# A hybrid decoder layer on one core: output projection at 512 columns, spread table building, gate weights through shared buffers, softmax division on ScalarE

## The chip, the cores and the metric

The kernel runs on one core of one Trainium2 chip. The metric is the device time in microseconds (us) of one execution, all loads and stores included. TensorE is the matmul engine, VectorE, ScalarE and GpSimd are the three elementwise engines, and SyncE (SP) issues the DMAs. The profile calls them PE (and PEld for its weight loads), DVE, ACT, POOL and SP.

## What is computed

The input x has 2048 positions of 1024 channels. It is normalised, projected to 2816 columns, worked on in three head groups, projected back with `w_out`, added to x and normalised again. Cut to what matters:

```python
hn = rmsnorm(x, norm_g)
a_in, a_gate, c_in, c_b, c_c, c_gate, q, q_gate = split(hn @ w_in)   # 384 x6, 256 x2
# A: 24 groups of a diagonal complex state-space model with 64 states, then GELU and a gated unit
s = associative_scan(lam_bar, b_bar @ a_in)
g = gelu(Re(C s) + d * a_in)
y_ssm = g * sigmoid(g @ w_glu + b_glu) * silu(a_gate)
# B: short causal convolution of width 3
y_conv = c_b * conv3(c_c * c_in) * silu(c_gate)
# M: attention of 4 heads of 64 into 256 memory rows
k, v = split(rmsnorm(mem, mem_norm_g) @ w_mem_kv)
y_mem = softmax(q k^T / 8) v * silu(q_gate)
h = x + concat(y_ssm, y_conv, y_mem) @ w_out                          # 1024 x 1024
out = rmsnorm(h, final_norm_g)
```

All data is float32. Matrix products are made from two-part operands: each operand is split into a rounded part (`hi`) and the rest (`lo`), and `mm3` (line 79) issues three matmuls: hi*hi, hi*lo and lo*hi.

## The kernel before, in words

**Quarters and stages.** The 2048 positions are cut into four quarters of 512. For each quarter `prep` (line 582) normalises x in four row blocks of 128 and transposes them into `hn`, channels on partitions. `proj` (line 606) makes one block of 128 output columns of the input projection: it loads a 1024 x 128 weight tile, splits it, and issues 8 x 3 matmuls with 512 columns (positions) into one PSUM tile. `ain`, `agate`, `qproj` and `conv` are loops over such blocks with their elementwise work. `attention(q, j)` (line 760) does two heads: scores into PSUM, row maximum on VectorE (line 778), exponential with a row sum on ScalarE (line 780), a reciprocal (line 782) and the division of the four 128 x 256 blocks by the row sum on VectorE (line 785), then transposes (line 795), the split into two parts, and the product with v (line 799). `ssm(hf)` (line 480) runs the state-space model over half the positions, eight steps of three groups each; its scan is a chain on VectorE that ends in `sC`, which TensorE reads at line 548. `glu(q)` (line 813) reads the result of `ssm` back from DRAM, splits it into `y_ssm`, and multiplies by `w_glu` in three column blocks of 128 (line 830). `outproj` and `outproj_last` (lines 893, 921) are the output projection.

**Output projection.** The weights of a matmul (stationary operand) are 128 positions of an output slice Y, its moving operand is a piece of `w_out`. `wout` (line 889) loads 512 rows x 256 columns of it and splits it. `outproj` loops over four column blocks, two halves of the rows, and four row blocks of positions; `omm` (line 866) then issues 4 k x 3 matmuls of 256 columns. Two PSUM tiles hold two row blocks each and are added to the reloaded x by VectorE (line 905). Quarters are finished in the order 1, 0, 3, 2. Quarter 2 comes last, in `outproj_last`, which loads all eight weight tiles ahead into buffers that have come free: three of the projections' buffers, the rest of `hn`'s, v's (`wvd`), a table's (`wtb`), and the conv and memory outputs' (`wyc`, `wym`). It does row blocks 0 and 1 together, then 2, then 3. Its conv and memory outputs have been reloaded from DRAM into `hn`'s buffer (`hy`, in `fetch_y`, line 848), as were those of quarter 0 into buffers of their own.

**Buffers.** `wtile` (line 127) loads a weight tile into a staging tile, rounds it on ScalarE (`split`, line 86) and makes the rest on GpSimd or VectorE (line 77). Staging `w` has two buffers, `wl`, the split weights, three. The tiles of `w_glu` are staged in the pair of buffers `ain`, which `glu` also uses for its input `gr`, and split into a buffer `wg` of its own, one deep. `xst` (tag `x`) holds two row blocks of x, and also the sets of turns below. PSUM has three tiles `mm`, two `tr`, one `po` (attention's product with v) and two `ss`, one bank each.

**Tables.** In the first quarter the kernel also builds the tables of the state-space model: four tables (`gen_table`, line 392, five steps each, six large VectorE operations) and eight sets of turns (`gen_turns`, line 442, one step each, six products and two sums on VectorE, then a store to `t_dram`). They follow `mem_rows` (four steps), which normalises the memory rows. Ahead of them `ssm_prologue` derives their parameters in many small operations.

**What sets the order.** The generators yield after each step, and `interleave(main, side, rate, start)` (line 676) advances `side` by `rate` steps for each step of `main`; `merge` does the same within one stream. This order gives each instruction its rank. A planner in the compiler then lays out each engine's instructions by rank and by its own estimate of when their inputs and buffers are ready. On the chip each engine and SP's queue run in that fixed order. Lines 1002 to 1026 write the stages out. The first quarter's: `agate(0)`, `qproj(0)`, `conv(0, 0)`, `conv(0, 1)` (15 steps) with `mem_rows` and all tables (32 steps) at a rate of 2.2, then `conv(0, 2)` and `memory_kv` with `prep(1)`.

Of the kernel before, what the change touches and what calls it, by code (L numbers as in the profile page):

```python
# [9 lines left out]
F32 = mybir.dt.float32  # L10
F32R = mybir.dt.float32r
# [34 lines left out]
def hymba_layer_kernel(  # L46
# [29 lines left out]
    def tt(o, a, b, op, e=V):  # L76
        e.tensor_tensor(o, a, b, op)  # L77
# [598 lines left out]
    def interleave(main, side, rate, start=0):  # L676
# [8 lines left out]
        for _ in side:  # L685
            pass

    def merge(a, b, rate):

        acc = 0.0  # L690
        for _ in a:
            yield
            acc += rate
            while acc >= 1.0:
                acc -= 1.0
                if next(b, 0) is None:
                    yield
        yield from b
# [61 lines left out]
    def attention(q, j):  # L760
# [5 lines left out]
        for ip in range(2):  # L766
# [15 lines left out]
            V.reciprocal(sm, sm)  # L782
            for a in range(2):
                for h in range(2):
                    V.tensor_scalar(pe[:, a, h], pe[:, a, h], sm[:, a, h:h + 1], None, ALU.mult)
                pes.append(pe[:, a])
            yield
        um = yv["pe"][:, 0].rearrange("p (a h m) -> p a h m", a=2, h=2)[:, :, 0]
# [24 lines left out]
    def glu(q):  # L813
# [13 lines left out]
            split(y_ssm[:, 0, t], y_ssm[:, 1, t], gr)  # L827
            yield
        for m in range(3):
            w = wtile(w_glu[0, :, m * P:(m + 1) * P], WS, P, f"wg{q}{m}", V, late["wg"], "a")  # L830
            ps = ps_ss.tile([P, QL], F32, tag="ss", name=f"psg{q}{m}")
            for k in range(3):
                mm3(ps, w[:, 0, k, :], w[:, 1, k, :], y_ssm[:, 0, k, :], y_ssm[:, 1, k, :], k == 0, k == 2)
            t_, g2 = (swk.tile([P, QL], F32, tag="pg", bufs=2, name=f"gt{q}{m}{z}") for z in range(2))
            S.activation(t_, ps, AF.Tanh, bias=bg[:, m:m + 1], scale=0.25)
            tt(g2, f32(y_ssm[:, 0, m, :]), f32(y_ssm[:, 1, m, :]), ALU.add, G)
            V.scalar_tensor_tensor(g2, t_, 1.0, g2, ALU.add, ALU.mult)
            V.scalar_tensor_tensor(us[m], g2, 0.125, us[m], ALU.mult, ALU.mult)
            yield
# [2 lines left out]
        yield  # L842


    yk = [("ssm", 0), ("ssm", 1), ("ssm", 2), ("conv", 0), ("conv", 1), ("mem", 0), ("mem", 1), ("conv", 2)]
    rows = [0, 1, 2, 3, 4, 6, 7, 5]

    def fetch_y(q):

# [13 lines left out]
                t = Y[q]["conv" if z + k < 3 else "mem"][:, :, (z + k) % 3]  # L863
                split(t[:, 0], t[:, 1], st[:, k], V if k else G)

    def omm(q, ps, i, kh, w, first):

        o_ = slice(i * P, (i + 1) * P)
        for k in range(4):
            nm, kk = yk[4 * kh + k]  # L870
            kr = rows[4 * kh + k] - 4 * kh
            mm3(ps, Y[q][nm][:, 0, kk, o_], Y[q][nm][:, 1, kk, o_], w[:, 0, kr, :], w[:, 1, kr, :],
                first and k == 0, kh == 1 and k == 3, skip_group_check=True)

    def residual(q, last=False):

# [9 lines left out]
                nc.sync.dma_start(h[z][u * NCH:(u + 1) * NCH], xq[q, u][:, 2 * z:2 * z + 2])  # L886
        return h

    def wout(q, n_, kh, dst=None, st="w", e=G):
        src = w_out[0, kh * 512:(kh + 1) * 512, n_ * 256:(n_ + 1) * 256]  # L890
        return wtile(src, 512, 256, f"wo{q}{n_}{kh}", e, dst, st)

    def outproj(q):
        h = residual(q)
        for n_ in range(4):
            ns = slice(n_ * 256, (n_ + 1) * 256)
            pss = [ps_mm.tile([P, 2, 256], F32, tag="mm", name=f"po{q}{n_}{b}") for b in range(2)]
            for kh in range(2):
                w = wout(q, n_, kh)
                for i in range(4):  # L900
                    omm(q, pss[i // 2][:, i % 2, :], i, kh, w, kh == 0 and i % 2 == 0)
                    yield
            for b in range(2):
                hb = h[b][:, :, ns]
                tt(hb, pss[b], hb, ALU.add)
        jk = tmp.tile([P, QL], F32, tag="ci", name=f"junk{q}")
        ss = sml.tile([P, 2, 4], F32, tag="ssf", name=f"ssf{q}")
        for i in range(4):
# [12 lines left out]
    def outproj_last(q):  # L921
# [4 lines left out]
        hg = late["big"].tile([P, 2, DM], F32, tag="big1", name="hg")  # L926

        def wv_(t):
            return t[:, :2 * 4 * 256].rearrange("p (z k n) -> p z k n", z=2, k=4)

        dsts = [None, None, None, Y[q]["rest"].rearrange("p z a (b n) -> p z (a b) n", b=2)]
        dsts.append(wv_(kvp.tile([P, 2 * 4 * 256], F32R, tag="vd", name="wvd")))
        dsts.append(wv_(stab.tile([P, GB * TW], F32, tag="tb", name="wtb").bitcast(F32R)))
        dsts.append(wv_(late["yc"].tile([P, 2 * 3 * QL], F32R, tag="yc", name="wyc")))
        dsts.append(wv_(late["ym"].tile([P, 2 * 2 * QL], F32R, tag="ym", name="wym")))
        ws = [[wout(q, n_, kh, dsts[2 * n_ + kh], "wx"[kh], V if kh else G) for kh in range(2)] for n_ in range(4)]
        ss, jk = (sml.tile([P, 4, 4], F32, tag=t_, bufs=1, name=t_) for t_ in ("ssl", "ssk"))

        def rstd(i, nss):
# [8 lines left out]
        for n_ in range(4):  # L948
            ns = slice(n_ * 256, (n_ + 1) * 256)
            ps = ps_mm.tile([P, 2, 256], F32, tag="mm", name=f"po{q}{n_}")  # L950
            for kh in range(2):
                for i in range(2):
                    omm(q, ps[:, i, :], i, kh, ws[n_][kh], kh == 0 and i == 0)
            for i in range(2):
                tt(h[i][:, ns], ps[:, i], h[i][:, ns], ALU.add)
                sumsq(h[i][:, ns], ss[:, i, n_:n_ + 1], junk[0][:, 0:256])
        for i in range(2):
            V.scalar_tensor_tensor(h[i], h[i], rstd(i, 4), fg_b, ALU.mult, ALU.mult)
            store(i, h[i])
        for i in range(2, 4):  # L960
            parts = [(0, 1), (2, 3)] if i == 2 else [(0, 1), (2,), (3,)]
            for b, ns_ in enumerate(parts):
                ns = slice(ns_[0] * 256, ns_[-1] * 256 + 256)
                ps = ps_mm.tile([P, 2, 256], F32, tag="mm", name=f"po{q}{i}_{b}")
                for a, n_ in enumerate(ns_):
                    for kh in range(2):
                        omm(q, ps[:, a, :], i, kh, ws[n_][kh], kh == 0 and a == 0)
                pv = ps.rearrange("p a n -> p (a n)")[:, :256 * len(ns_)]
                tt(h[i][:, ns], pv, h[i][:, ns], ALU.add)
                sumsq(h[i][:, ns], ss[:, i, b:b + 1], junk[1][:, :256 * len(ns_)])  # L970
# [10 lines left out]

    def open_left():
        phs.close()
        for n_ in ("yc", "ym", "wg"):
            late[n_] = ctx.enter_context(tc.tile_pool(name=n_, bufs=1, reuse_waits="tile"))

    prologue = ssm_prologue()
# [15 lines left out]
    open_right()  # L1003
    load_small()
    gens = chain(*[z for b in range(NB) for z in (gen_table(b), gen_turns(2 * b), gen_turns(2 * b + 1))])
    kv = memory_kv()
    interleave(chain(agate(0), qproj(0), conv(0, 0), conv(0, 1)), chain(mem_rows(), gens), 2.2)
    open_left()
    interleave(merge(conv(0, 2), kv, 0.7), prep(1), 2.0, 4)
    interleave(ain(1), chain(attention(0, 0), attention(0, 1)), 2.5)  # L1010

    def main(q):
# [43 lines left out]
```

## Time and profile before

| what | us |
|---|---|
| median of 3 runs | 902.94 (900.92 to 909.04) |
| the profiled execution | 904.45 |
| its span, first to last instruction | 902.5 |
| TensorE busy in the span | 843.1 |
| VectorE busy | 613.7 |
| ScalarE busy | 367.0 |
| GpSimd busy | 301.7 |

Times in rows are microseconds from the span's start unless marked ns. `x24` after a group is its number of instructions; what follows the bar is busy time and the mean ns of one, then the engine's idle time just before them and what ended it. Matmuls overlap in their pipeline, so the duration of one is longer than the distance to the next start.

### The profile page before, as it was taken

The numbers are of one execution on the slowest core, as the hardware profiler recorded it, in microseconds if no ns is written. First come the engines' busy times: TensorE is split into PE (matmuls) and PEld (weight loads), VectorE is DVE, ScalarE is ACT, GpSimd is POOL, SyncE is SP. The second block draws the span as 40 slices with busy tenths as digits, with TensorE's granted clock in tenths as the row PEclk, the third lists the DMA queues.
The fourth block names the chain that finished last, engine by engine and source line by source line (L and its number), as shares of the span: only waits on it lengthen the run. The fifth ranks groups of instructions, "written<-read, shape, count | busy, mean of one in ns | idle before, by whom it ended". The sixth has DMA issues, their size and how long they took to land. (4 is left out here: it accounts for less than half of the span.)

```text
span 902.5 us, 13173 instructions
## 1 busy us (share of the span) xinstructions
PE 843.1 (93%) x4876; PEld 723.7 (80%) x4876; DVE 613.7 (68%) x1244; ACT 367.0 (41%) x706; POOL 301.7 (33%) x157
## 2 busy tenths in 40 slices
PE   2998999889998998999999899999999998989996
PEld 2985777778877877899888688899878876879996
DVE  6898899583998896936434664344399996865353
ACT  5343433545343434433444533335233344444511
POOL 2000001154222344444545434334443343455400
PEclk9999899999997999999999999999999999999999
DMA  9553649966464534454575632656757744493362
GB/s 205 161 150 103 189 131 269 267 187 201 125 179 130 156 93 119 108 152 141 159 239 150 160 114 84 161 165 186 214 156 207 211 128 125 117 222 112 125 177 57
DMA packets 180647, 142.97 MB, mean 158 GB/s; under 512 B 41192, under 2 KB 164584, under 8 KB 180584
## 3 DMA queue, kind: packets, MB, share of 16 engines
q1 hardware_dynamic: 180584, 142.14, 56.4%
q8 instruction: 38, 0.62, 0.3%
q14 instruction: 25, 0.20, 0.1%
HBM read 113.80 MB, written 26.74 MB: 156 GB/s over the span
## 5 line engine op out<-in xcount | busy, mean ns | idle before, releaser
L77 POOL TENSOR_TENSOR wo<-wo_st,wo 128x1024 fp32r<-128x1024 f32 x26 | 63.8, 2454 | 70.6 <-ACT wo L86 59.2
L77 DVE TENSOR_TENSOR h<-po,h 128x512 f32<-128x512 f32 (+1 forms) x37 | 22.2, 615 | 43.5 <-PE po L83 34.5
L81 PE MATMUL po<-wo,yssm 128*128 128x256 f32 x168 | 48.5, 289 | 1.8 <-ACT yssm L86 1.8
L83 PE MATMUL po<-wo,yssm 128*128 128x256 f32 x168 | 48.2, 287 | 0.0
L82 PE MATMUL po<-wo,yssm 128*128 128x256 f32 x168 | 47.8, 285 | 0.0
L780 ACT ACTIVATE pe<-sps,nm 128x256 f32<-128x256 f32 x64 | 29.5, 472 | 39.4 <-DVE nm L778 35.1
L81 PE MATMUL psai<-hn,wai 128*128 128x512 f32 (+1 forms) x120 | 42.7, 362 | 2.8 <-ACT hn L86 2.1
L82 PE MATMUL psai<-hn,wai 128*128 128x512 f32 (+1 forms) x120 | 42.5, 356 | 0.3 <-DVE hn L77 0.2
L83 PE MATMUL psai<-hn,wai 128*128 128x512 f32 (+1 forms) x120 | 42.0, 353 | 0.0
L81 PE MATMUL pscg<-hn,wcg 128*128 128x512 f32 x96 | 39.8, 415 | 2.2 <-ACT wcg L86 2.2
L86 ACT CAST wo<-wo_st 128x1024 fp32r<-128x1024 f32 x27 | 28.2, 1044 | 33.3 <-PE po L83 16.2
L81 PE MATMUL po<-wo,yconv 128*128 128x256 f32 x144 | 40.7, 283 | 0.0
L83 PE MATMUL po<-wo,yconv 128*128 128x256 f32 x144 | 40.3, 280 | 0.0
L82 PE MATMUL po<-wo,yconv 128*128 128x256 f32 x144 | 40.1, 279 | 0.0
L83 PE MATMUL pscg<-hn,wcg 128*128 128x512 f32 x96 | 39.1, 407 | 0.5 <-DVE wcg L77 0.5
L81 PE MATMUL psag<-hn,wag 128*128 128x512 f32 x96 | 39.5, 411 | 0.0
L82 PE MATMUL pscg<-hn,wcg 128*128 128x512 f32 x96 | 39.0, 407 | 0.0
L77 POOL TENSOR_TENSOR wcb<-wcb_st,wcb 128x1024 fp32r<-128x1024 f32 x9 | 22.9, 2550 | 47.9 <-ACT wcb L86 47.9
L83 PE MATMUL psag<-hn,wag 128*128 128x512 f32 x96 | 38.5, 401 | 0.0
L82 PE MATMUL psag<-hn,wag 128*128 128x512 f32 x96 | 38.4, 400 | 0.0
L81 PE MATMUL pscb<-hn,wcb 128*128 128x512 f32 x96 | 38.3, 399 | 0.0
L81 PE MATMUL psci<-hn,wci 128*128 128x512 f32 x96 | 38.3, 399 | 0.0
(710 smaller groups left out, 2903.5 us busy)
## 6 DMA issues: line engine op xcount, KB each, us to landing
wo_st<-in_w_out_dram SPq DMA_DIRECT2D x32, 512.0 KB, 3.8
tb<-t_dram SPq DMA_DIRECT2D x16, 960.0 KB, 5.5
out_dram<-h SPq DMA_DIRECT2D x32, 256.0 KB, 3.4
h<-in_x_dram SPq DMA_DIRECT2D x14, 512.0 KB, 7.4
wai_st<-in_w_in_dram SPq DMA_DIRECT2D x12, 512.0 KB, 4.3
wag_st<-in_w_in_dram SPq DMA_DIRECT2D x12, 512.0 KB, 4.3
wci_st<-in_w_in_dram SPq DMA_DIRECT2D x12, 512.0 KB, 4.2
wcc_st<-in_w_in_dram SPq DMA_DIRECT2D x12, 512.0 KB, 4.1
```

Of the source, the lines that this page charges most:

```text
L77: e.tensor_tensor(o, a, b, op)
L81: T.matmul(ps, lh, rh, start=first, stop=False, **kw)
L82: T.matmul(ps, lh, rl, start=False, stop=False, **kw)
L83: T.matmul(ps, ll, rh, start=False, stop=last, **kw)
L86: S.copy(hi, src)
L780: S.activation(pe[:, a, h], sps[h][:, a], AF.Exp, bias=nm_[:, a, h:h + 1], accum_out=sm[:, a, h:h + 1])
```

## The change

Four edits. The output projection works with 512 columns and 256 rows of `w_out` per tile, in four row pairs taken in the order 0, 1, 3, 2, with four accumulators (three `mm`, one `po`); the last quarter likewise, except that its very last column half stays in two pieces of 256. The division of the softmax is an ACTIVATE on ScalarE. `w_glu` comes in two tiles, of 256 and 128 columns, through staging `w` and buffers `wl`. The tables go alongside the first four main pieces at a rate of 1.5 instead of 2.2; the rest runs at 0.9 beside `conv(0, 2)` and `memory_kv`, where `prep(1)` runs too, and what is left of it follows `prep(1)`.

```diff
+    def weave(main, side, rate):
+        acc = 0.0
+        for _ in main:
+            acc += rate
+            while acc >= 1.0:
+                acc -= 1.0
+                next(side, None)
+            yield
...
-                    V.tensor_scalar(pe[:, a, h], pe[:, a, h], sm[:, a, h:h + 1], None, ALU.mult)
+                    S.activation(pe[:, a, h], pe[:, a, h], AF.Copy, scale=sm[:, a, h:h + 1])
...
         for m in range(3):
-            w = wtile(w_glu[0, :, m * P:(m + 1) * P], WS, P, f"wg{q}{m}", V, late["wg"], "a")
+            if m % 2 == 0:
+                c1 = min(m * P + 256, WS)
+                wg = wtile(w_glu[0, :, m * P:c1], WS, c1 - m * P, f"wg{q}{m}", V)
+            w = wg[:, :, :, m % 2 * P:m % 2 * P + P]
...
-    yk = [("ssm", 0), ("ssm", 1), ("ssm", 2), ("conv", 0), ("conv", 1), ("mem", 0), ("mem", 1), ("conv", 2)]
-    rows = [0, 1, 2, 3, 4, 6, 7, 5]
+    yk = [("ssm", 0), ("ssm", 1), ("ssm", 2), ("conv", 0), ("conv", 1), ("conv", 2), ("mem", 0), ("mem", 1)]
+    pairs = (0, 1, 3, 2)
...
-    def omm(q, ps, i, kh, w, first):
+    def omm(q, ps, i, kp, w, cs=slice(0, 512)):
         o_ = slice(i * P, (i + 1) * P)
-        for k in range(4):
-            nm, kk = yk[4 * kh + k]
-            kr = rows[4 * kh + k] - 4 * kh
-            mm3(ps, Y[q][nm][:, 0, kk, o_], Y[q][nm][:, 1, kk, o_], w[:, 0, kr, :], w[:, 1, kr, :],
-                first and k == 0, kh == 1 and k == 3, skip_group_check=True)
+        for k in range(2):
+            nm, kk = yk[2 * kp + k]
+            mm3(ps, Y[q][nm][:, 0, kk, o_], Y[q][nm][:, 1, kk, o_], w[:, 0, k, cs], w[:, 1, k, cs],
+                kp == pairs[0] and k == 0, kp == pairs[-1] and k == 1)
...
-    def wout(q, n_, kh, dst=None, st="w", e=G):
-        src = w_out[0, kh * 512:(kh + 1) * 512, n_ * 256:(n_ + 1) * 256]
-        return wtile(src, 512, 256, f"wo{q}{n_}{kh}", e, dst, st)
+    def wout(q, nh, kp, dst=None, st="w", e=G):
+        src = w_out[0, kp * 256:(kp + 1) * 256, nh * 512:(nh + 1) * 512]
+        return wtile(src, 256, 512, f"wo{q}{nh}{kp}", e, dst, st)
...
-        for n_ in range(4):
-            ns = slice(n_ * 256, (n_ + 1) * 256)
-            pss = [ps_mm.tile([P, 2, 256], F32, tag="mm", name=f"po{q}{n_}{b}") for b in range(2)]
-            for kh in range(2):
-                w = wout(q, n_, kh)
+        for nh in range(2):
+            ns = slice(nh * 512, (nh + 1) * 512)
+            pss = [ps_mm.tile([P, 512], F32, tag="mm", name=f"po{q}{nh}{b}") for b in range(3)]
+            pss.append(ps_po.tile([P, QL], F32, tag="po", name=f"po{q}{nh}3"))
+            for kp in pairs:
+                w = wout(q, nh, kp)
                 for i in range(4):
-                    omm(q, pss[i // 2][:, i % 2, :], i, kh, w, kh == 0 and i % 2 == 0)
+                    omm(q, pss[i], i, kp, w)
                     yield
-            for b in range(2):
-                hb = h[b][:, :, ns]
-                tt(hb, pss[b], hb, ALU.add)
+            for i in range(4):
+                hb = h[i // 2][:, i % 2, ns]
+                tt(hb, pss[i], hb, ALU.add)
...
-        for n_ in ("yc", "ym", "wg"):
+        for n_ in ("yc", "ym"):
...
-    kv = memory_kv()
-    interleave(chain(agate(0), qproj(0), conv(0, 0), conv(0, 1)), chain(mem_rows(), gens), 2.2)
+    side = chain(mem_rows(), gens)
+    for _ in weave(chain(agate(0), qproj(0), conv(0, 0), conv(0, 1)), side, 1.5):
+        pass
+    interleave(weave(merge(conv(0, 2), memory_kv(), 0.7), side, 0.9), prep(1), 2.0, 4)
+    for _ in side:
+        pass
     open_left()
-    interleave(merge(conv(0, 2), kv, 0.7), prep(1), 2.0, 4)
```

`outproj_last` is changed in the same way: weight tiles of 256 x 512 into the same eight buffers, two column halves for row blocks 0 and 1, and for row block 3 the pieces 0 to 512, 512 to 768 and 768 to 1024.

## Rows read from the trace of the kernel before

**Rows 1.** The page, part 1: busy us, share of the span, instructions.
```profile
PE 843.1 (93%) x4876; PEld 723.7 (80%) x4876; DVE 613.7 (68%) x1244; ACT 367.0 (41%) x706; POOL 301.7 (33%) x157
```

**Rows 2.** Who waited for whom, TensorE: total us, times, longest.
```profile
PE ps_y L548 <- DVE sC L77: 9.9, 6, 3.1
PE psg L81 <- ACT wg L86: 8.0, 4, 3.4
PE trq L144 <- DVE hn L77: 4.1, 2, 2.8
PE psqg L81 <- DVE uq L619: 4.1, 1, 4.1
PE pscg L81 <- ACT wcg L86: 2.2, 1, 2.2
...
PE po L81 <- ACT yssm L86: 1.8, 1, 1.8
```

**Rows 3.** Order of time, TensorE, 377 to 383: start, duration, line, tiles.
```profile
378.07 0.39 PE L83 MATMUL pscg<-hn,wcg 128*128 128x512 f32 x1
...
380.79 0.39 PE L83 MATMUL pscg<-hn,wcg 128*128 128x512 f32 x1
381.01 0.28 PE L81 MATMUL po<-wo,yssm 128*128 128x256 f32 x1
...
382.33 0.28 PE L83 MATMUL po<-wo,yssm 128*128 128x256 f32 x1
```

**Rows 4.** Order of time, TensorE, 842 to 850, in the last stage.
```profile
843.16 0.28 PE L83 MATMUL po<-wo,yconv 128*128 128x256 f32 x1
...
845.20 0.28 PE L83 MATMUL po<-wo,ymem 128*128 128x256 f32 x1
...
849.45 0.28 PE L81 MATMUL po<-wo,hy 128*128 128x256 f32 x1
...
849.69 0.28 PE L83 MATMUL po<-wo,hy 128*128 128x256 f32 x1
```

**Rows 5.** Stretches: length, busy PE, PEld, DVE, ACT, POOL, clock, DMA share, GB/s.
```profile
80.00:100.00 20.00, 14.66 (x79) 10.12 (x79) 14.84 (x51) 7.80 (x13) 1.10 (x2) 0.74 0.57 137
150.00:200.00 50.00, 44.85 (x253) 38.36 (x253) 37.32 (x70) 23.50 (x48) 18.79 (x10) 0.97 0.86 232
200.00:220.00 20.00, 20.00 (x100) 16.29 (x99) 5.90 (x16) 10.36 (x25) 8.04 (x4) 1.00 0.81 235
270.00:290.00 20.00, 16.88 (x76) 14.29 (x75) 17.72 (x40) 8.67 (x23) 3.76 (x2) 0.74 0.47 134
760.00:810.00 50.00, 44.08 (x239) 37.05 (x235) 32.94 (x42) 23.82 (x44) 27.31 (x15) 0.93 0.68 168
```

**Rows 6.** VectorE by line and shape: count, busy us, mean ns, idle before.
```profile
L785 DVE TENSOR_SCALAR pe<-pe,sm 128x256 f32<-128x256 f32 x64 | 29.4, 524 | 0.2
...
L77 DVE TENSOR_TENSOR ge<-t0e,t1e 128x384 f32<-128x384 f32 x16 | 9.8, 652 | 0.6 <-DMA t_dram<-ge 0.5
...
L77 DVE TENSOR_TENSOR t0e<-s_U,s_W 128x256 f32<-128x256 f32 x24 | 8.7, 415 | 0.5 <-ACT s_W L330 0.5
...
L77 DVE TENSOR_TENSOR gt<-gt 128x768 f32<-128x768 f32 x8 | 7.5, 954 | 0.0
```

**Rows 7.** Line 785: count, then minimum, median and maximum ns.
```profile
L785 DVE TENSOR_SCALAR pe<-pe,sm x64: 341/349/2544, 206.6 to 769.6; 128x256 f32<-128x256 f32 x64
```

**Rows 8.** ScalarE by line and shape, 845 to the end.
```profile
L101 ACT ACTIVATE junkci<-h 128x256 f32<-128x256 f32 x8 | 3.3, 418 | 11.9 <-DVE h L77 11.7
```

**Rows 9.** Order of time, ScalarE, 760 to 766.
```profile
763.07 0.62 ACT L86 CAST yssm<-gr 128x512 fp32r<-128x512 f32 x1 [3.08 <-DMA gr<-g_dram]
763.63 0.51 ACT L86 CAST wg<-wg_st 128x384 fp32r<-128x384 f32 x1
```

**Rows 10.** Order of time, DMA issues on SP, 795 to 806.
```profile
797.43 2.01 SPq L823 DMA_DIRECT2D us<-y_dram  x3
799.53 4.23 SPq L131 DMA_DIRECT2D wg_st<-in_w_glu_dram  x2
```

More of the change, by code (lines that the diff above doesn't have):

```diff
@@ L928, in wv_ @@
         def wv_(t):
-            return t[:, :2 * 4 * 256].rearrange("p (z k n) -> p z k n", z=2, k=4)
-        dsts = [None, None, None, Y[q]["rest"].rearrange("p z a (b n) -> p z (a b) n", b=2)]
-        dsts.append(wv_(kvp.tile([P, 2 * 4 * 256], F32R, tag="vd", name="wvd")))
+            return t[:, :2 * 2 * 512].rearrange("p (z k n) -> p z k n", z=2, k=2)
+        dsts = [None, None, None, Y[q]["rest"]]
+        dsts.append(wv_(kvp.tile([P, 2 * 2 * 512], F32R, tag="vd", name="wvd")))
         dsts.append(wv_(stab.tile([P, GB * TW], F32, tag="tb", name="wtb").bitcast(F32R)))
@@ L935, in outproj_last @@
         dsts.append(wv_(late["ym"].tile([P, 2 * 2 * QL], F32R, tag="ym", name="wym")))
-        ws = [[wout(q, n_, kh, dsts[2 * n_ + kh], "wx"[kh], V if kh else G) for kh in range(2)] for n_ in range(4)]
+        ws = [{kp: wout(q, nh, kp, dsts[4 * nh + a], "wx"[a % 2], V if a % 2 else G) for a, kp in enumerate(pairs)}
+              for nh in range(2)]
         ss, jk = (sml.tile([P, 4, 4], F32, tag=t_, bufs=1, name=t_) for t_ in ("ssl", "ssk"))
@@ L947, in outproj_last @@
         junk = [tmp.tile([P, QL], F32, tag=t_, name="junk" + t_) for t_ in ("ci", "u")]
[L948 to L951, printed above, removed]
+        for nh in range(2):
+            ns = slice(nh * 512, (nh + 1) * 512)
+            pss = [ps_mm.tile([P, 512], F32, tag="mm", name=f"po{q}{nh}{i}") for i in range(2)]
+            for kp in pairs:
                 for i in range(2):
-                    omm(q, ps[:, i, :], i, kh, ws[n_][kh], kh == 0 and i == 0)
+                    omm(q, pss[i], i, kp, ws[nh][kp])
@@ L954, in outproj_last @@
             for i in range(2):
-                tt(h[i][:, ns], ps[:, i], h[i][:, ns], ALU.add)
-                sumsq(h[i][:, ns], ss[:, i, n_:n_ + 1], junk[0][:, 0:256])
+                tt(h[i][:, ns], pss[i], h[i][:, ns], ALU.add)
+                sumsq(h[i][:, ns], ss[:, i, nh:nh + 1], junk[0])
         for i in range(2):
-            V.scalar_tensor_tensor(h[i], h[i], rstd(i, 4), fg_b, ALU.mult, ALU.mult)
+            V.scalar_tensor_tensor(h[i], h[i], rstd(i, 2), fg_b, ALU.mult, ALU.mult)
@@ L959, in outproj_last @@
             store(i, h[i])
         for i in range(2, 4):
[L961 to L970, printed above, removed]
+            parts = [(0, 512), (512, 1024)] if i == 2 else [(0, 512), (512, 768), (768, 1024)]
@@ L971, in outproj_last @@
+            for b, (c0, c1) in enumerate(parts):
+                ns = slice(c0, c1)
+                ps = ps_mm.tile([P, 512], F32, tag="mm", name=f"po{q}{i}_{b}")[:, :c1 - c0]
+                for kp in pairs:
+                    omm(q, ps, i, kp, ws[c0 // 512][kp], slice(c0 % 512, c0 % 512 + c1 - c0))
+                tt(h[i][:, ns], ps, h[i][:, ns], ALU.add)
+                sumsq(h[i][:, ns], ss[:, i, b:b + 1], junk[1][:, :c1 - c0])
                 tt(hg[:, i - 2, ns], h[i][:, ns], fg_b[:, ns], ALU.mult)
```

## The prediction, made before the changed kernel was run

> **What bounds the kernel now.** I read the page's busy times first, then who waits for whom on TensorE, then its order of time, then busy times by stretch. The page gives TensorE 843.1 of 902.5 us busy and VectorE 613.7 [rows 1]. So only three things move the end: matmul time, TensorE's idle time, and time at the half clock that follows idling. The reader is to see in the waits that no single stall is large: VectorE's scan chain costs 9.9 us in six waits, the gate weights 8.0 in four, one projection 4.1, and TensorE waits on two other ScalarE casts for 2.2 and 1.8 [rows 2]. The mean of a matmul there overlaps its neighbours, so matmul cost is taken from differences of start times [rows 3, 4]. The stretches then say which engine was full beside a stall, and what the granted clock was, a mean over time at 2.4 GHz and, after a stall, at 1.2 [rows 5].
>
> The profiled execution took 904.45 us with a span of 902.5; the median of the three runs is 902.94, that is 1.5 less. Terms are summed against 904.45 and the sum is carried over to the median.
>
> **512 columns.** In rows 3 a 512-column matmul starts every 0.2267 us: 12 steps from 378.07 to 380.79. A 256-column one with the S5 outputs as weights starts every 0.120 us: 11 steps from 381.01 to 382.33. With the conv or memory outputs of the odd quarters the last stage shows 0.1133, 18 steps from 843.16 to 845.20, and with the reloaded ones of quarter 2 again 0.120, two steps from 849.45 to 849.69 [rows 4]. Two of 0.1133 are just one of 512 columns; two of 0.120 are 13.3 ns more. The code has 4 quarters x 4 column blocks x 4 row blocks x 8 k x 3 = 1536 narrow matmuls. S5 outputs feed 576 of them, quarter 2's reloaded outputs 240; some 96 of these, whose output weights lie in the old conv and memory tiles, I count as 0.1133. That leaves 720, or 360 pairs x 13.3 ns = 4.8 us gained. The other pairs gain nothing. Ends: 0, if the wide matmul runs at the 0.235 that neighbours can cause (an estimate from the spread of steps between 0.1133 and 0.120), and 6.
>
> Beside that figure: the Trainium skill ("TensorE: Matmul & The Clock Gate", Back-to-back issue gap) gives a matmul at the full clock its columns at 2.4 GHz plus some 2.5 ns, so a pair would save 2.5 ns and 768 pairs 1.9 us as an estimate. The trace's narrow step differs with the operands, which a fixed cost per matmul does not give, so the rows decide.
>
> The first weight tile of quarter 1's projection now uses two k for four row blocks, so 12 matmuls on S5 slice 0 take 2.7 us where they took 1.44. The wait of 1.8 us for the split of a later slice [rows 2] shrinks by 1.3. Take -1.3 (ends -1.8 and 0).
>
> Weight traffic stays at eight tiles of 512 KB a quarter, each feeding 24 x 0.2267 = 5.4 us instead of 48 x 0.12 = 5.8. Four accumulators are held instead of two, so a new column half needs bank 0 free. Row block 0 is done 18 matmuls, 4.1 us, before row block 3, and one eviction takes about 0.69 us on a VectorE that is not full in these stages: 0, with 3 as the bad end if VectorE is late at each boundary.
>
> **Softmax division.** 64 VectorE instructions go, 29.4 us busy, 524 ns in the mean [rows 6] with 349 as median and 2544 at most [rows 7]. The nearest row on ScalarE, 128x256 within SBUF, takes 418 ns [rows 8], so 26.8 us arrive on an engine that is busy 8.7 of 20 us in the stretch from 270 on [rows 5]. VectorE sheds them where it binds: from 270 to 290 it is busy 17.7 of 20 us while TensorE waits for the scan chain, and the granted clock is 0.74 [rows 5]. The half clock there is worth up to 0.26 x 20 = 5.2, so the waits of 9.9 and this make 15.1 at most. Each attention call takes 8 x 0.524 = 4.2 us off VectorE, more than the longest wait of this kind. But half of the calls lie beside no scan stage, and the dependent chain itself is not shortened. I take -6. The bad end is +8: ScalarE now waits for the reciprocal sixteen times with casts and PSUM reads queued behind it, which could treble the 4.0 us that TensorE loses to its other casts [rows 2].
>
> The long divisions are as long as a GpSimd split of a weight tile. The Trainium skill ("SBUF — State Buffer", SBUF: two separate sides) says that VectorE and GpSimd share a port pair that one instruction holds to its end, and that ScalarE never waits there. By that rule the excess over the median, 64 x 0.175 = 11.2 us, leaves VectorE with the rest; it is already inside the 524 used above.
>
> **Gate weights.** Now two tiles (256 and 128 columns) go through the projections' staging and weight buffers, where three went through a one-deep buffer. At stake are 8.0 us of waits [rows 2] and the half clock between 760 and 810, where the mean is 0.93, so 0.07 x 50 = 3.5 [rows 5]: 11.5 at most. Next late is the S5 result: at 763.07 ScalarE was still splitting the last slice, which came by DMA, just before the weights [rows 9]. Early weights free only the matmuls on slices 0 and 1, 6 x 0.2267 = 1.4 us a call. In the last gate the weight loads were issued at 799.53, behind three loads of the gate that began at 797.43 on SP's queue [rows 10], and that order stays. I take -4. The bad end is +7: staging has two buffers and weights three, and a gate tile held over two steps leaves projections two; eight extra tiles could each cost about 0.9.
>
> **Tables.** Ten of 32 side steps move behind the third convolution block: the fourth table, four of eight sets of turns, one end of a table. From rows 6 a table is six operations of about 0.954 us and about 1 of small ones, 6.7; a set of turns is six of 0.415 and two of 0.652, 3.8. Moved: 6.7 + 15.2 = 21.9 us of VectorE. From 150 to 200 it is idle 12.7 us of 50, from 200 to 220 another 14.1 of 20 [rows 5], and some 6 us of this work ran after 150 already, so it fits, with little to spare before the second quarter's rows are wanted. What it may take away is the stretch 80 to 100: a wait of 4.1 for a projection's eviction, and a clock of 0.74, worth up to 5.2. That eviction stood behind a set of turns, but also behind the prologue's last small operations, whose memory it reuses and which the change does not shorten. I take -2 (ends -9.3 and +25).
>
> **Sum.** -4.8 - 1.3 + 0 - 6 - 4 - 2 = -18.1. 904.45 becomes 886.3, and the median 902.94 becomes 884.8. The order on every engine is laid out by a planner with its own costs, so some small new stall is likely; I add 1.2 for it and say 886.
>
> **Rivals.**
> - Nearly every wait named goes, since taking work off VectorE and unblocking TensorE help each other: -4.8 - 1.3 - 15.1 - 11.5 - 9.3 = -42.0, that is 861; with a tenth left of the waits, 865. For it: VectorE is nearly full wherever the scans stall. Against it: the chains' latency stays.
> - The shared weight buffers starve the projections: +7 in place of -4, 897. For it: the same two staging buffers already serve every projection. Against it: from 200 to 220 TensorE is busy all the time and GpSimd, which empties them, 8.0 of 20 us [rows 5].
> - ScalarE's new waits delay its casts: +8 in place of -6, 900. For it: ScalarE is a strict queue and a reciprocal may stand behind a scan. Against it: it is idle about half or more of every stretch in [rows 5].
> - Slower: the moved tables stand in VectorE's queue ahead of the second quarter's rows, and there TensorE has nothing else, since the next projections need all four row blocks. The moved sets of turns also hold the two buffers into which these rows are loaded. Price: 21.9 us of VectorE less what of it finds idle time early, with half clock of 5.2 as in 80 to 100: up to 27, so 884.8 + 2 + 27 = 914. It turns the whole into a loss from 20 us of new wait between 170 and 215, and into a loss of over 1% from 29. For it: two waits for such splits stand in the view already, 4.1 us together [rows 2]. Against it: 26.8 us of idle VectorE up to 220.
>
> **How the numbers follow.** Forecast 0.54 (its own range 878 to 894); nearly all waits gone 0.10; buffers 0.12; ScalarE 0.11; tables 0.13, of which most ends above 903. About 1%, 9 us, is what a measurement of this kernel tells from no change, so faster means under 894 and slower over 912. Faster: all but little of the forecast, all of the second, a fifth of the two that meet at 897 to 900: 0.65. Slower: most of the last and a share for two mishaps at once: 0.12. Same: 0.23. The range runs from 868, leaving out half of the best case, to 908, leaving out most of the slower one.
>
> **What would show it.** Output matmuls at 512 columns with steps of 0.227 to 0.229 and some 744 of them; the rest, 48, at 256. Scan waits on TensorE down from 9.9 to about 5. Gate-weight waits from 8.0 to 4 or less, with no new row for a projection's cast above 3. VectorE about 30 us less busy, ScalarE about 25 more. No wait over 4 us between 80 and 100. I am wrong if TensorE's idle time is not at least 8 us smaller, or if a wait of over 5 us stands before the second quarter's first projections.

## The result and the profile after

The changed kernel took 913.63 us (median of 4 runs, 911.17 to 914.95) against 903.68 for the kernel before (4 runs): a ratio of 1.0100, with a 95% interval from 1.0066 to 1.0134. The change makes it slower. The prediction said 886 and a range up to 908, so it was wrong in sign and outside its range. The profiled execution took 911.17 us, with a span of 909.4.

The page's busy times of after, which answer to [rows 1]:

```profile
PE 841.1 (92%) x4132; PEld 687.8 (76%) x4132; DVE 602.2 (66%) x1172; ACT 389.8 (43%) x758; POOL 301.4 (33%) x157
```

TensorE's busy time hardly changed. Its idle time did: span less busy was 902.5 - 843.1 = 59.4 us and is 909.4 - 841.1 = 68.3. Who waited for whom on TensorE in after, to be held against [rows 2] (total us, times, longest). Both lists leave out their first row, the wait for the very first rows of x, which hardly changed (10.8 before, 10.6 in after):

```profile
...
PE po L809 <- DVE pT L77: 7.2, 4, 3.9
PE psqg L81 <- DVE uq L619: 4.5, 1, 4.5
PE trq L144 <- DVE hn L77: 4.1, 1, 4.1
PE trq L144 <- DVE xb L602: 3.1, 2, 2.6
PE pscc L81 <- ACT wcc L86: 3.0, 1, 3.0
PE po L809 <- ACT pT L86: 2.9, 1, 2.9
PE ps_y L548 <- DVE sC L77: 2.7, 3, 1.6
PE psv L82 <- POOL wv L77: 2.7, 1, 2.7
PE po L81 <- DVE q22a L77: 2.5, 1, 2.5
PE po L82 <- POOL wo L77: 2.0, 2, 1.3
PE psk L83 <- POOL wk L77: 1.9, 1, 1.9
PE tr_m L419 <- DVE hn L77: 1.8, 1, 1.8
...
PE psk L81 <- ACT wk L86: 1.2, 1, 1.2
```

The reader is to see an exchange. The gate's 8.0 us are gone and the scan's 9.9 are down to 2.7, as hoped. In their place stand waits that before had hardly or not at all: attention's product `po` for its split (7.2 and 2.9), a projection for its weights (`wcc`, 3.0), the output projection behind VectorE and for its own weights (`q22a` and `wo`, 2.5 and 2.0), and a group of small ones that all lie between 168 and 202 us: `xb`, `wv`, `wk` twice and `tr_m`, together 10.7. The stretches of after show where they bite, against [rows 5] (length, busy PE, PEld, DVE, ACT, POOL, clock, DMA share, GB/s):

```profile
80.00:100.00 20.00, 15.17 (x81) 10.20 (x81) 14.30 (x52) 8.00 (x13) 1.10 (x2) 0.83 0.57 140
150.00:200.00 50.00, 40.34 (x221) 35.16 (x219) 34.23 (x71) 21.35 (x43) 18.22 (x10) 0.93 0.80 210
200.00:220.00 20.00, 18.91 (x100) 13.82 (x101) 6.65 (x15) 10.31 (x23) 4.76 (x2) 1.00 0.74 221
270.00:290.00 20.00, 17.63 (x93) 14.25 (x92) 19.69 (x40) 10.25 (x29) 3.66 (x2) 0.88 0.68 206
760.00:810.00 50.00, 45.01 (x204) 35.96 (x204) 34.99 (x40) 28.87 (x54) 25.92 (x14) 0.97 0.51 129
```

From 150 to 200 TensorE works 4.5 us less than before, although VectorE is idle there for 15.8 us, 3.1 more than before, and from 200 to 220 another 1.1 less. The other three stretches are a little better. The same can be read from when stages begin on TensorE (first matmul of each, from the order of time; quarters count from 0):

| TensorE begins | before | after | after later by |
|---|---|---|---|
| first memory key | 163.9 | 160.4 | -3.5 |
| quarter 1's first projection | 198.8 | 205.0 | 6.2 |
| quarter 1's q | 216.9 | 226.4 | 9.5 |
| output of quarter 1 | 381.0 | 390.7 | 9.7 |
| output of quarter 0 | 578.3 | 587.6 | 9.3 |
| output of quarter 3 | 791.3 | 801.2 | 9.8 |
| output of quarter 2 | 848.4 | 856.5 | 8.1 |
| the last matmul | 893.7 | 900.9 | 7.2 |

Some 13 us are lost between the memory keys and quarter 1's q, where the moved tables are, and 2.6 are won in the last two output projections. In between, gains and losses nearly cancel. So there were two questions: how the tables lose 13 us beside an idle VectorE, and where the gains of the other three edits went.

### The profile page after: what moved, and what is told of

Same layout as the page of the kernel before. It is cut to its first block, busy times and chain, and to the rows that moved or that the text cites. A ratio compares the mean times of both kernels' runs of the same rounds, so it can differ in the third digit from the quotient of the medians.

```text
span 909.4 us, 11645 instructions
## 1 busy us (share of the span) xinstructions
PE 841.1 (92%) x4132; PEld 687.8 (76%) x4132; DVE 602.2 (66%) x1172; ACT 389.8 (43%) x758; POOL 301.4 (33%) x157
## 5 line engine op out<-in xcount | busy, mean ns | idle before, releaser
L81 PE MATMUL pscc<-hn,wcc 128*128 128x512 f32 x96 | 39.3, 409 | 3.0 <-ACT wcc L86 3.0
L77 POOL TENSOR_TENSOR wci<-wci_st,wci 128x1024 fp32r<-128x1024 f32 x9 | 22.5, 2501 | 52.9 <-ACT wci L86 52.6
L77 DVE TENSOR_TENSOR hn<-trq,hn 128x512 fp32r<-128x512 f32 x32 | 21.5, 682 | 26.4 <-ACT hn L86 26.4
L83 PE MATMUL pscc<-hn,wcc 128*128 128x512 f32 x96 | 38.5, 401 | 0.2 <-POOL wcc L77 0.2
L82 PE MATMUL pscc<-hn,wcc 128*128 128x512 f32 x96 | 38.6, 402 | 0.0
L81 PE MATMUL pscg<-hn,wcg 128*128 128x512 f32 x96 | 38.5, 401 | 0.0
L83 PE MATMUL psci<-hn,wci 128*128 128x512 f32 x96 | 37.9, 394 | 0.6 <-POOL wci L77 0.6
L81 PE MATMUL psci<-hn,wci 128*128 128x512 f32 x96 | 38.4, 400 | 0.0
L81 PE MATMUL pscb<-hn,wcb 128*128 128x512 f32 x96 | 38.1, 397 | 0.0
L83 PE MATMUL pscg<-hn,wcg 128*128 128x512 f32 x96 | 38.0, 396 | 0.0
L83 PE MATMUL pscb<-hn,wcb 128*128 128x512 f32 x96 | 37.9, 394 | 0.0
L82 PE MATMUL pscg<-hn,wcg 128*128 128x512 f32 x96 | 37.9, 394 | 0.0
L82 PE MATMUL psci<-hn,wci 128*128 128x512 f32 x96 | 37.8, 394 | 0.0
```

What stands on the lines that cost most here:

```text
L81: T.matmul(ps, lh, rh, start=first, stop=False, **kw)
L82: T.matmul(ps, lh, rl, start=False, stop=False, **kw)
L83: T.matmul(ps, ll, rh, start=False, stop=last, **kw)
```

## The experiments

### Each edit alone

Four kernels carry one hunk group of the change's diff each on the kernel before, and one the change without its table hunk. The groups by their telling line:

```diff
 tables_alone    + interleave(weave(merge(conv(0, 2), memory_kv(), 0.7), side, 0.9), prep(1), 2.0, 4)
 out512_alone    + src = w_out[0, kp * 256:(kp + 1) * 256, nh * 512:(nh + 1) * 512]
 soft_alone      + S.activation(pe[:, a, h], pe[:, a, h], AF.Copy, scale=sm[:, a, h:h + 1])
 gate_alone      + wg = wtile(w_glu[0, :, m * P:c1], WS, c1 - m * P, f"wg{q}{m}", V)
 all_but_tables  the change with the old order of the tables
```

> The changed kernel with the old order of the tables (all 32 side steps beside the first 15 main steps at a rate of 2.2); the other three edits stay. Theory 1, the tables' new place costs the time: from the third convolution block's end to the second quarter's first query projection the changed kernel took 66.0 us (160.4 to 226.4) and the kernel before 53.0 (163.9 to 216.9), 13 more, and it had gained 3.5 ahead of that. So this one is about 9.5 us faster than the changed kernel, 904, and the stretch is back at 53 to 55. Theory 2, the other edits or the planner's reordering of everything cost it: the time stays above 909, and the stretch alone gets shorter while others lengthen.

> The kernel before with the new order of the tables alone. Theory 1: the loss is here already, 8 to 13 us, 911 to 916, with TensorE waiting 10 us or more between the first memory-key matmul and the second quarter's first projection. Theory 2, the loss comes only with the other edits: 900 to 906.

> The kernel before with the output projection at 512 columns alone. By the steps of the two traces (0.117 us for 256 columns in the mean, 0.2285 for 512) 744 wide ones save some 4 us, and the first wait of quarter 1's projection 1 more: 898 to 900. Rival, what is gained is given back at the accumulators: new waits on VectorE's additions or on the weight tile's split cost 4 or more, so 903 to 906.

> The kernel before with the softmax division on ScalarE alone. My theory: VectorE's scan waits on TensorE fall from 9.9 us to 3 to 5, as the changed kernel shows 2.7, and 5 to 8 us are gained, 896 to 899. Rival, ScalarE's queue gives it back: waits for the split of the transposed softmax and for ScalarE's casts grow by as much (7.2 and 2.9 us stand there in the changed kernel, where it was 1.9 and 1.7), so 901 to 906.

> The kernel before with the gate's weights in two tiles through the projections' staging and weight buffers. The output projection alone gave about -10 us and the softmax division alone about -4, but both with the gate only -3 against runs of the kernel before: some +11 are to be found. Theory G, the shared buffers cost it: this run is slower by 3 to 8, 908 to 913, with new waits of projections for their weights or of the gate for its tile in the stages with a gate. Theory O, the first two edits remove the same waits and the gate is neutral: 901 to 907, the gate's waits gone and others in their place. Theory I, only the gate with the softmax division loses (ScalarE's divisions stand ahead of the gate's casts): faster alone, 896 to 902.

| kernel | median us | ratio to before (95%) |
|---|---|---|
| tables_alone | 914.62 | 1.0115 (1.0084 to 1.0146) |
| out512_alone | 895.45 | 0.9898 (0.9865 to 0.9930) |
| soft_alone | 900.71 | 0.9964 (0.9942 to 0.9986) |
| gate_alone | 909.00 | 1.0016 (0.9984 to 1.0049) |
| all_but_tables | 902.84 | 0.9965 (0.9939 to 0.9991) |

Of 905.5 us these are +10.4, -9.2, -3.3 and +1.4. The tables alone lose as much as the whole change. But the four sum to -0.7, and the change is at +9.0: about 10 us of the gains are gone in the combination. The three without the tables sum to -11.1 and measured -3.2 together, so most of that, 8 us, is lost without the tables too. The interval of `gate_alone` includes no change at all.

In the profile of `all_but_tables` the stretch from the first memory key to quarter 1's q takes 52.1 us (164.1 to 216.3), as in the kernel before (53.0; after 66.0), which bears out theory 1. `out512_alone` gained more than either theory had allowed. `soft_alone` ended between its two, and its profile shows scan waits of 7.9 us, not 3 to 5: the 2.7 of after is not the softmax edit's work alone.

### What in the tables costs

In after, DMA issues on SP around the second quarter's rows:

```profile
159.82 4.81 SPq L434 DMA_DIRECT2D gt<-s_Kp  x6
164.73 0.53 SPq L131 DMA_DIRECT2D wk_st<-in_w_mem_kv_dram  x1
...
167.94 1.26 SPq L439 DMA_DIRECT2D t_dram<-gt  x2
...
173.56 1.15 SPq L572 DMA_DIRECT2D xb<-in_x_dram  x2
...
175.54 1.15 SPq L572 DMA_DIRECT2D xb<-in_x_dram  x2
```

The same queue in the kernel before:

```profile
140.31 1.24 SPq L439 DMA_DIRECT2D t_dram<-gt  x2
...
146.44 1.17 SPq L572 DMA_DIRECT2D xb<-in_x_dram  x2
...
148.29 0.59 SPq L572 DMA_DIRECT2D xb<-in_x_dram  x1
```

Row blocks 1 and 3 of the second quarter (`xb`) are loaded into the buffer of the third table. That table was stored at 140 and is now stored at 168, so the two blocks load some 27 us later. And ScalarE's order in after:

```profile
166.37 1.55 ACT L436 COPY gt<-gt 128x768 f32<-128x768 f32 x1 [8.22 <-DMA gt<-s_Kp]
168.93 1.04 ACT L86 CAST wk<-wk_st 128x1024 fp32r<-128x1024 f32 x1 [1.02 <-DMA wk_st<-in_w_mem_kv_dram]
```

It stands 8.22 us at the table's last copy, which waits for the table's eight small DMAs; the second memory key's weight cast is behind it. VectorE at the same rows in after:

```profile
183.22 1.09 DVE L77 TENSOR_TENSOR t0e<-s_U,s_W 128x256 f32<-128x256 f32 x3
184.23 1.09 DVE L77 TENSOR_TENSOR t1e<-s_U,s_W 128x256 f32<-128x256 f32 x3
185.24 2.31 DVE L77 TENSOR_TENSOR q11a<-q11a,q11v 128x1 f32<-128x1 f32 x1
...
188.87 1.27 DVE L602 SCALAR_TENSOR_TENSOR xb<-xb,q11o,ng_b 128x1024 f32<-128x1024 f32 x1
...
197.77 3.27 DVE L602 SCALAR_TENSOR_TENSOR xb<-xb,q13o,ng_b 128x1024 f32<-128x1024 f32 x1
```

Once the rows are late, the last sets of turns are ahead of them on VectorE, and the fourth block is normalised at 201. So three causes were possible: the buffer (B), ScalarE's queue (Q), VectorE's moved work (V). Four kernels on `tables_alone` tell them apart.

```diff
 tab_copy_on_vector
-        S.copy(s["T"].rearrange(...), Tq.rearrange(...))
+        V.tensor_copy(s["T"].rearrange(...), Tq.rearrange(...))
 tab_row_own_buffer
-        xb = more_rows(q) if q == 1 else []
+        xb = [fg_b] if q == 1 else []
-                xt = xb[i // 2] if xb and i % 2 else xst.tile(...)
+                xt = xb[0] if xb and i == 1 else xst.tile(...)
 tab_six_turns
+        if b > 5:
+            yield
+            return
+        for d_ in (5, 6, 7) if b == 5 else (b,):
```

`tab_both` has the first two. `tab_six_turns` leaves out the last two sets of turns and stores the sixth in their place.

> The new table order alone (914.6 us against 905) with one thing changed: the copy of a finished table's third section (line 436), which waits for the table's eight small DMAs, goes to VectorE. Three theories of why the new order costs about 9.5 us. Q, ScalarE's queue: ScalarE stood 7.9 us at this copy, with the second memory key's weight cast, the convolution step and the last gate's cast behind it. By Q the casts come 3 to 5 us earlier, TensorE's waits for wk (1.7 and 1.9) and for wv (3.4) mostly go, and the time is 908 to 911. B, the buffer: two of the second quarter's four row blocks are loaded into the buffer of the third table, which is stored only at 169 us where it was 140, so they load at 174.7 where they did at 148. By B the loads stay within 1.5 us of 174.7 and the time stays within 2 us of 914.6. V, VectorE: the last two sets of turns (7.6 us) stand at 184 to 190 in front of the row blocks; by V this edit adds 1.5 us to VectorE and nothing is gained: 914 to 916.

> The new table order alone, but the second quarter's row blocks no longer use a table's buffer: block 1 is loaded into the final norm's vector tile, which is idle then (that vector is loaded after the rows), and block 3 follows block 0 through the two-deep row buffer. B, the buffer: block 1 is loaded before 150 and normalised before 180, the projection that began at 207.8 begins near 200, and the time is 905 to 909. Q, ScalarE's queue at the table's copy: that wait of 7.9 and the waits for wk and wv stay, so at most 3 us are gained, 911 to 915. V, VectorE: rows that are ready sooner also stand ahead of the last turns here, so V expects a gain too, of up to 6: 908 to 912, but only as far as VectorE is full between 180 and 200 now and is not after.

> Both edits: the table's copy on VectorE and the second quarter's rows out of the table's buffer. If Q and B each hold a part of the 9.5 us, this takes nearly all of it: 903 to 907. If B alone holds it, as the row's own buffer alone (905 to 909), and if Q alone, as the copy on VectorE alone (908 to 911). If the cost is VectorE's moved work itself, 910 to 914.

> The new table order alone, with the last two of eight sets of turns left out (the sixth is stored in their place, with two stores more), so 7.6 us of VectorE's work is gone from between 180 and 190, ahead of the row blocks. The buffers and the copy on ScalarE are as in the new order. V, VectorE's moved work is what delays the rows: row block 1 is normalised about 5 to 7 us earlier than 190.8, and the time is 907 to 910. B, the buffer: block 1 cannot be normalised before it lands, near 180, and block 3 later still, so 2 to 5 us are gained: 910 to 913. Q, ScalarE's queue: nothing at the memory keys; 912 to 915.

| kernel | median us | ratio to before (95%) |
|---|---|---|
| tab_copy_on_vector | 912.87 | 1.0078 (1.0063 to 1.0093) |
| tab_row_own_buffer | 906.52 | 1.0015 (0.9996 to 1.0034) |
| tab_both | 903.52 | 0.9979 (0.9965 to 0.9993) |
| tab_six_turns | 908.96 | 1.0031 (1.0005 to 1.0058) |

The buffer holds most of it: about 9 of the 10.4 us go when the rows leave the table's buffer. VectorE in `tab_row_own_buffer`:

```profile
164.01 1.28 DVE L602 SCALAR_TENSOR_TENSOR fg_b<-fg_b,q11o,ng_b 128x1024 f32<-128x1024 f32 x1
...
188.69 1.28 DVE L602 SCALAR_TENSOR_TENSOR xq<-xq,q13o,ng_b 128x1024 f32<-128x1024 f32 x1
...
195.42 1.04 DVE L77 TENSOR_TENSOR ge<-t0e,t1e 128x384 f32<-128x384 f32 x2
```

Against `tables_alone` (190.8 and 199.7), block 1 is taken up 27 us sooner and block 3 eleven sooner, and the turns have dropped behind them. TensorE begins quarter 1 at 197.8, even a little ahead of the kernel before. In `tab_copy_on_vector` the two blocks are still asked for at 173.9 and 175.8, as B had it, and the time stays above Q's range. ScalarE's queue is worth some 3 us (with the buffer mended, 1.0015 becomes 0.9979).

Leaving out two sets of turns gave 908.96, in V's range and a little better than B had allowed. By the ratios it wins 7.6 us where the buffer wins 9.0, and their intervals overlap, so the times alone do not tell V from B. The traces tell more: TensorE begins quarter 1 at 207.8 in `tables_alone`, at 204.3 without the two sets, and at 197.8 with the buffer, although VectorE has all the turns still to do there. So the turns do delay the rows, but where late rows let them go first. V is a link of B's chain more than a rival, and these runs don't give the turns a price of their own. With both faults mended the new order is better than the old, by 0.1 to 0.4%.

### Where the other gains went

`out512_gate` and `out512_soft` are pairs of edits with the old tables. Two kernels more split the gate's edit on `out512_alone`: both keep three tiles of 128 columns and share one thing with the projections.

```diff
 out512_gate_staging
-            w = wtile(w_glu[...], WS, P, f"wg{q}{m}", V, late["wg"], "a")
+            w = wtile(w_glu[...], WS, P, f"wg{q}{m}", V, late["wg"], "w")
 out512_gate_buffers
+            w = wtile(w_glu[...], WS, P, f"wg{q}{m}", V, None, "a")
```

> Output projection at 512 columns and gate weights in the shared buffers, no softmax edit, old tables. G: the gate's loss on top of -10, so 899 to 904. O: the gate is neutral, 893 to 897. I: the gate's own gain on top of -10, 887 to 893.

> Output projection at 512 columns and softmax division on ScalarE, without the gate's edit, old tables. G: the two gains add up, 888 to 893. O: they overlap, and it stands where the three together stood, 899 to 903. I: the gains add up here, 888 to 893, and it is the pair with the gate that loses.

> Output projection at 512 columns; the gate's weights in three tiles as before, staged in the projections' two staging buffers, split into the gate's own buffer. If the shared staging is what takes the 10 us (output and input projection weights wait on SP for a staging buffer, and the row loads behind them), 902 to 907 as with both. If the shared split buffers are, 893 to 898.

> The other half: the gate's weights in three tiles staged as before, split into the projections' three buffers. If the shared split buffers are what takes the 10 us (the casts of the next projections wait for a free one), 902 to 907. If the staging is, 893 to 898, and perhaps less, as the gate's waits of 5 us for its own one-deep buffer should shrink.

| kernel | median us | ratio to before (95%) |
|---|---|---|
| out512_gate | 906.39 | 1.0007 (0.9983 to 1.0032) |
| out512_soft | 896.93 | 0.9908 (0.9872 to 0.9944) |
| out512_gate_staging | 921.05 | 1.0191 (1.0159 to 1.0224) |
| out512_gate_buffers | 903.65 | 0.9995 (0.9968 to 1.0021) |

The gate's edit takes back all that the output projection gives, and the shared split buffers alone nearly as much. Sharing the staging alone costs 26 us against `out512_alone`, far more than the whole edit with its two tiles. The runs were to tell one half from the other as the cause, and both lose. What the gate's edit does is seen in `gate_alone`, TensorE's waits:

```profile
PE po L799 <- DVE pT L77: 6.3, 4, 2.2
...
PE pscc L81 <- ACT wcc L86: 2.8, 1, 2.8
...
PE po L799 <- DVE pe L77: 1.9, 1, 1.9
...
PE psg L81 <- ACT yssm L86: 1.4, 1, 1.4
```

The gate no longer waits for its weights, only for the S5 result, which the prediction had named as next late. A projection waits for its own instead, late in quarter 3. Its `wcc` was asked for on SP at 754.63:

```profile
754.63 0.37 SPq L131 DMA_DIRECT2D wcc_st<-in_w_in_dram  x1
```

and in the kernel before at 734.95:

```profile
734.95 0.37 SPq L131 DMA_DIRECT2D wcc_st<-in_w_in_dram  x1
```

Such a tile takes 4.3 us in the median to land in `gate_alone`, so by this estimate it was there near 759. It was cast only at 773.51, because ScalarE's queue stood at the S5 result ahead of it. ScalarE in `gate_alone`:

```profile
772.51 0.62 ACT L86 CAST yssm<-gr 128x512 fp32r<-128x512 f32 x1 [6.29 <-DMA gr<-g_dram]
...
773.51 1.05 ACT L86 CAST wcc<-wcc_st 128x1024 fp32r<-128x1024 f32 x1
```

And `po` waits for splits that VectorE does late. VectorE in `gate_alone`, at the first of these waits:

```profile
361.52 2.35 DVE L77 TENSOR_TENSOR q21a<-q21r 128x1 f32<-128x1 f32 x1 [1.69 <-POOL q21r L77]
...
367.50 1.29 DVE L602 SCALAR_TENSOR_TENSOR xq<-xq,q21o,ng_b 128x1024 f32<-128x1024 f32 x1
368.70 1.28 DVE L77 TENSOR_TENSOR pT<-trp,pT 128x512 fp32r<-128x512 f32 x2
```

ScalarE had finished `pT`'s casts by 362.6, but a row block of the next quarter is ahead of the split on VectorE's queue, whose own chain goes back and forth with GpSimd. That block feeds nothing that is due soon; `pT` holds TensorE. The order put it there, not the load on any engine. That these weights come later, and that their cast stands behind another wait, is shown by the rows; that the order changed because the buffers are shared is an inference. `out512_gate_buffers` loses nearly as much with no wait for `wcc` at all, so this one wait is not the whole cause, and what makes the staging alone so costly was not settled.

### Mended versions

`best_guess` has the output projection, the softmax and the mended tables, `out512_mended` the first and the last of these, `after_mended` the whole change with mended tables.

> Output projection at 512 columns, softmax division on ScalarE, and the new table order with both of its faults mended (rows out of the table's buffer, the table's copy on VectorE); the gate as before. The mended order was 2 to 3 us better than the kernel before. By G and I 886 to 891, better than every version so far; by O 897 to 901. The second quarter's first projection should begin near 197, as in the mended order, and the last stage take about 42 us instead of 45.4.

> The full change with both faults of its table order mended (rows out of the table's buffer, the table's copy on VectorE). If they are all of what the table order loses, this is where the change without the table order stood, 902.8, or 2 to 3 us better as the mended order was against the kernel before: 899 to 903. If the order loses something else beside the other edits, 906 to 912.

> Output projection at 512 columns and the mended table order, softmax and gate as before. If gains add up, 895.5 less 2 to 3: 892 to 894. If they overlap, as the softmax edit did with the output projection, 895 to 900.

| kernel | median us | ratio to before (95%) |
|---|---|---|
| best_guess | 901.10 | 0.9955 (0.9930 to 0.9981) |
| after_mended | 906.68 | 1.0022 (0.9992 to 1.0053) |
| out512_mended | 896.72 | 0.9919 (0.9887 to 0.9950) |

The mend gives the change 7 of its 9 us back. It ends some 5 us above `all_but_tables` by the ratios, not below it, so the new order loses something else beside the other edits, which was not found. On `out512_alone` neither the mended tables nor the softmax add anything. The best version is the 512-column output projection by itself, 0.9898; the other edits on top of it cost nothing at best. In `best_guess` quarter 1's first projection began at 196.1, as expected, but the last stage took 45.8 us, not 42.

## Why the prediction was wrong

**512 columns: right mechanism, nearly the right size.** In after the wide matmul steps as forecast, here with the reloaded outputs of quarter 2 in the last stage, 15 steps of 0.2267 us:

```profile
864.44 0.39 PE L81 MATMUL po<-wtb,hy 128*128 128x512 f32 x1
...
867.84 0.39 PE L82 MATMUL po<-hy 128*128 128x512 f32 x1
```

The term was -6.1 with the first weight tile, and the edit alone measured -9.2 (-12.2 to -6.3 by its interval); its profiled execution took 897.70 us and has a span 6.6 us shorter than before. The size was nearly right, but not by the parts that were added. By the mean steps, 0.117 us for 256 columns in the kernel before and 0.2285 to 0.229 for 512, the matmuls gain some 3.5 to 4 us (an estimate), not 4.8. The wait for `yssm` is 1.8 (1.3 forecast). The prediction left out what follows that wait: from 386 to 392 the kernel before has a granted clock of 0.72 in the mean, and from 386.6 to 389.9 its 256-column matmuls step at 0.21 us, the half clock (1.2 GHz). `out512_alone` has no wait there and 1.00 from 385 to 391. By an estimate that is worth 0.28 x 6 = 1.7 us more. The gate's waits also fell, from 8.0 to 5.3, without the gate's edit. Against these stands a cost that was set at 0 with 3 as the bad end: the accumulators wait for VectorE at two column boundaries.

```profile
PE po L81 <- DVE h L77: 3.5, 2, 1.8
```

From their first matmul to their last, the four output stages are 5.3 us shorter there: 3.1 in quarter 1, 0.1 in quarter 0, 2.0 in the last two together. The Trainium skill's rule ("TensorE: Matmul & The Clock Gate", Back-to-back issue gap), 1.9 for all pairs, lies further off than the rows.

**Softmax: half the size.** The term was -6; alone the edit gives -3.3, and nothing on top of the output projection. The scan waits, which were to halve, fall from 9.9 to 7.9 in `soft_alone`. ScalarE's side was priced well: 27.3 us arrive (26.8 forecast), and its waits for the reciprocal are only 4.2 in all. The line of after:

```profile
L795 ACT ACTIVATE pe<-pe,sm 128x256 f32<-128x256 f32 x64 | 27.3, 500 | 4.2 <-DVE sm L792 4.2
```

VectorE was expected to lose some 30 us of busy time. In `soft_alone` it loses 613.7 - 593.4 = 20.3. The rest comes back on other instructions. One scan product on VectorE in the kernel before, and then in `soft_alone` (count, busy us, mean ns, idle before):

```profile
L77 DVE TENSOR_TENSOR m<-m,tb 128x384 f32<-128x384 f32 x16 | 14.8, 923 | 0.3
```

```profile
L77 DVE TENSOR_TENSOR m<-m,tb 128x384 f32<-128x384 f32 x16 | 20.7, 1295 | 0.4
```

So 9.1 of 29.4 us stayed, not far from the 11.2 by which the divisions stood over their median and which the prediction had put down to GpSimd. It let them leave with the divisions. Not every neighbour grew: the scan itself fell from 33.1 to 26.7. The rows read as if the waiting moves between VectorE's instructions, which no run here isolates. The prediction also took 0.524 us for the cost of one division; these durations overlap, and by the row's busy time it is 29.4 / 64 = 0.46, so 3.7 us a call and not 4.2.

**Gate: the term that failed second.** The forecast was -4, measured +1.4 alone, which is not clear of no change, and +10 beside the output projection. The waits for `wg` went from 8.0 to none, better than forecast. But the second rival had the sign: shared buffers that delay the projections, priced at +7 in place of -4. Its mechanism is shown only in part, by one projection's weights that came 20 us later, and the cause of the rest stays open. Against it stood that TensorE was busy all through 200 to 220 [rows 5], which is not where a gate runs.

**Tables: the step that failed.** The prediction put it as 21.9 us of VectorE that "fits, with little to spare before the second quarter's rows are wanted". It was right that VectorE had the time. But idle time of an engine was taken for the limit, where the limit was a buffer: the third table's store frees the place into which two row blocks are loaded, and a store that comes 28 us later loads them 27 us later. The prediction had the step in its list of what moves, as "one end of a table", and counted only its work on VectorE. The tables' term of -2 measured +10.4 alone, and some +12 beside the other three edits (from -3.2 to +9.0).

The slower rival had the place and the sign, and even a shared buffer, though the wrong one: it named the pair that the turns use, but the row blocks that go through that pair were asked for at 148 and 157 in after, earlier than the 164 to 169 of the kernel before. That its time, 914, is the measured 913.6 is luck: its 27 us of loss are more than twice too many, and the -16.1 of the other terms that it kept came to -3.2. Its two thresholds do not follow from its own sum either: with 886.8 to start from, a loss begins at 16 us of new wait, not 20, and one of over 1% at 25, not 29. It got 0.13 since only VectorE's idle time was weighed against it.

**The sum.** The terms were added up, with 1.2 for all small new stalls. The runs show that they do not add: four edits of -0.7 together make +9.0. Each edit changes the order on every queue. The tables' loss is shown to be of that kind; that the rest is too was only argued.

**What was to show it.** Steps at 512, the count of 256-column matmuls (48), gate waits under 4 and scan waits down came true. VectorE 30 less busy did not, nor did "no wait over 4 between 80 and 100": the wait of `psqg` for `uq` is still there and is 4.5, where it was 4.1. Of the two signs named for being wrong, the first was there in full: TensorE's idle time is 8.9 us larger, not 8 smaller. The second, a wait of over 5 before the second quarter, came as six waits under 3 us.

## What to carry to other kernels

Before work is moved, list what its last instruction releases (buffers, and the loads that go into them), and follow those loads to who needs them; an idle engine on the way says nothing about that chain. Price a shared buffer also by the tiles that are then asked for later, not by the wait that goes alone. And measure edits alone and in pairs where a planner lays out the order: their gains do not add, and the best kernel here was one edit of four.

## What was not expected of the hardware

A VectorE instruction on one element per partition can take as long as a GpSimd split. VectorE in `out512_gate`:

```profile
409.92 2.33 DVE L77 TENSOR_TENSOR q22a<-q22r 128x1 f32<-128x1 f32 x1 [0.66 <-POOL q22r L77]
412.17 0.68 DVE L77 TENSOR_TENSOR h<-po,h 128x512 f32<-128x512 f32 x1
```

and GpSimd in the same stretch:

```profile
409.89 2.34 POOL L77 TENSOR_TENSOR wo<-wo_st,wo 128x1024 fp32r<-128x1024 f32 x1
```

The square of one number per partition starts 0.03 us after the split of a weight tile and ends with it; in the same trace, with GpSimd idle, such instructions take 0.14 to 0.16. An eviction that TensorE waits for 3.6 us stands behind it. The Trainium skill ("SBUF — State Buffer", SBUF: two separate sides) describes the shared port pair as a lock that one instruction holds to its end, and counts VectorE instructions with two SBUF inputs among those that need it; this trace agrees, 2.33 beside 2.34 us. So row statistics, tiny as they are, are poor neighbours for weight splits.
